# Input projection in 256-column units with seven half-size products for eight, and gates by exponential and logarithm

## The chip, the cores and the metric

One core of a Trainium2 chip runs the whole program. The metric is the device time of one execution in microseconds (us); three runs of the kernel before gave 1003.85, 1004.28 and 1004.38, median 1004.28.

Five engines run side by side, each in the order of its own queue: TensorE (PE, matmuls, with its weight loads shown as PEld), VectorE (DVE), ScalarE (ACT), GpSimd (POOL) and SyncE (SP), which issues most of the DMAs. Matmuls write to PSUM, eight banks of 128 x 512 float32 values; everything else lies in SBUF.

## The reference

One decoder layer on x of 512 tokens x 2048 columns, in float32. Sixteen heads of width 128 in three kinds: six forgetting (FoX), six stick-breaking, four differential ones with two maps each.

```
h = x @ w_in                      # 2048 x (16 heads x 4 x 128 + 6): q, k, v, gate of each head
FoX:            softmax(q k / sqrt(128) + c_t - c_s) v,  c = cumsum(log_sigmoid(ff + b_f))
stick-breaking: weights exp(log_beta + later sums of log(1 - beta)), strictly causal, times v
differential:   (softmax(q1 k1 - slope*dist) - lam * softmax(q2 k2 - slope*dist)) v, RMS norm
out = concat(heads * silu(gate)) @ w_out
x   = LayerNorm(2**0.25 * x + out) * ln_g + ln_b
```

## The kernel before, in words

Every product of two float32 matrices is made of three float32r passes (`mm3`, L104): each operand is split into a high and a low part (`split`, L113: ACT casts the high part, DVE subtracts it for the low part), and high x high, high x low, low x high are summed in PSUM.

The input projection runs over 16 column groups of 512 columns, for each quad of heads one with q and k of two heads, one with the values of four, one with the other q and k, one with four gates. A group runs over 8 weight chunks of two row tiles (256 x 512 values, `load_chunk`, L144), and a chunk over four accumulators (one PSUM bank each, tags `pj0` to `pj3`): this is a unit, 2 x 3 matmuls of 512 columns. For q, k and gates the weights are the stationary operand and x^T (`xh`, `xl`) is the moving one; for values it is the other way round, so that they come out by tokens.

The order of PE is the order of emission (`mm` pins it). Other work is put between units by a clock that counts them: `at_unit` (L175) files a step under a unit, `tick` (L178) runs what is due. `attend` (L595) files each head's steps: for the four blocks of 128 queries the scores (two PSUM tiles `psL`), eight to ten units later the transposes of the weights through the one PSUM tile `psT` (`transpose_w`, L536, evacuated by an ACT cast `pth` and a DVE subtraction `ptl`), then the weighted sum over values into the one tile `psO` (`weighted_v`, L548). Evacuations of a finished accumulator belong to `evac_qk`, `evac_diff`, `evac_v` and `evac_g`. The gate there is g / (1 + exp(-g)), with four reciprocals of 128 columns per head on DVE (L411). The engines other than PE get their order from a scheduler that lays the instructions out on an estimated timeline.

Weights are split two chunks ahead (`AHEAD`), through four raw tiles and three pairs of split tiles. Twelve of the sixteen gated heads go to DRAM and are read back during the last group (`load_mix`, L443). The output projection (four groups of 512 columns, the last one in another order so that the norms can start early) and the layer norm end the program.

Of the kernel before, what the change touches and what calls it, by code (L numbers as in the profile page):

```python
# [63 lines left out]
UNITS = NK // KC * 4        # matmul units (one accumulator, one weight chunk) in a column group  # L64
NRES = 3
AHEAD = 2                   # weight chunks split ahead of their products
# [3 lines left out]
def trunk(ctx, tc, x, w_in, b_f, lam_p, subln_g, w_out, ln_g, ln_b, out):  # L70
# [33 lines left out]
    def mm3(ps, ah, al, bh, bl, first, last, part=None):  # L104
        """ps += a^T b in three float32r passes, or one of them."""
# [6 lines left out]

    def split(hi, lo, src, scale=None):  # L113
        """hi + lo = src (* scale), each with at most 12 significant bits."""
        if scale is None:
            A.copy(hi, src)  # L116
            V.tensor_tensor(out=lo, in0=src, in1=hi.bitcast(F32), op=ALU.subtract)  # L117
# [8 lines left out]
    groups = []  # L126
    for quad in range(4):
        hq = ORDER[4 * quad:4 * quad + 4]
        for kind in ("qk", "v", "qk", "g"):
            if kind == "qk":  # L130
                hs = hq[:2] if len(groups) % 4 == 0 else hq[2:]
                cols = [head_cols(h)[0] for h in hs] + [head_cols(h)[1] for h in hs]
            else:
                hs = hq
                cols = [head_cols(h)[2 if kind == "v" else 3] for h in hs]
            groups.append((kind, hs, cols))
    NG = len(groups)
    NJ = NK // KC
    chunks = [(w1, g, j) for g in range(NG) for j in range(NJ)]
    chunks += [(w2, g, j) for g in range(NG, NG + 4) for j in range(NJ)]  # L140
    ready = {}
    RES = (NG + 3) * NJ + NRES       # from here on the parts stay resident

    def load_chunk(n):  # L144
        """Load and split rows of KC k-tiles of a column group's weights."""
        w, g, j = chunks[n]
        raw = wpool.tile([P, KC, 512], F32, tag="raw", bufs=4, name=f"raw{n}")
        if w is w1:
            for dst, src, wd in runs(groups[g][2]):
                nc.sync.dma_start(raw[:, :, dst:dst + wd], w[:, j * KC:(j + 1) * KC, src:src + wd])  # L150
        else:
            k0, c0 = ORDER[j * KC], (g - NG) * 512
            nc.sync.dma_start(raw, w[:, k0:k0 + KC, c0:c0 + 512])
        if n < RES:
            hi = wpool.tile([P, KC, 512], F32R, tag="whi", bufs=3, name=f"whi{n}")
            lo = wpool.tile([P, KC, 512], F32R, tag="wlo", bufs=3, name=f"wlo{n}")
        else:
            hi = fin.tile([P, KC, 512], F32R, name=f"whi{n}")
            lo = fin.tile([P, KC, 512], F32R, name=f"wlo{n}")
        if n < RES and not (j == AHEAD and g < NG):  # L160
            split(hi, lo, raw)
        else:
            pin(A.copy(hi, raw))
            pin(V.tensor_tensor(out=lo, in0=raw, in1=hi.bitcast(F32), op=ALU.subtract))
        ready[n] = (hi, lo)
# [17 lines left out]
    def run_group(g, acc, product, evac, after_chunk=None):  # L183
        """All units of a column group: product(n, kt, accumulator), then evac of each accumulator."""
        for j in range(NJ):
            n = g * NJ + j
            if n == 0:
                load_chunk(AHEAD)
                for k in range(KC):
                    for part in range(3):  # L190
                        for c in range(4):
                            if k == KC - 1 and part == 2:
                                tick()
                            product(ready[n], k, k, c, part)
                        if k == 0 and part == 0:
                            transpose_x(1)
                        if k == 1 and part < 2:
                            transpose_x(2 + part)
            for c in range(4) if n > 0 else ():
                if c == 0 and n + AHEAD < len(chunks) and n + AHEAD not in ready:  # L200
                    load_chunk(n + AHEAD)
                tick()
                for k in range(KC):
                    product(ready[n], k, j * KC + k, c)
                if j == NJ - 1:
                    evac(c, acc[c])
            del ready[n]
            if after_chunk is not None:
                after_chunk(j)

# [5 lines left out]
    # products of ones, read by nobody: they open TensorE's clock gate while the first loads run  # L216
# [10 lines left out]
    xh = [kx.tile([P, S], F32R, tag=f"h{kt}", name=f"xh{kt}") for kt in range(NK)]  # L227
    xl = [kx.tile([P, S], F32R, tag=f"l{kt}", name=f"xl{kt}") for kt in range(NK)]
# [4 lines left out]
    with ExitStack() as actx:  # L233
        at = actx.enter_context(tc.tile_pool(name="at", bufs=1))

        def wk(name):
            return at.tile([P, S], F32, tag="wk", bufs=8, name=name)
# [5 lines left out]
        xv = xf.rearrange("(tb p) c -> p tb c", p=P)  # L243
        xraw = []

        def load_x(c):
            xr = at.tile([P, NT, 512], F32, tag=("pth", "ptl")[c % 2], name=f"xr{c}")
            xraw.append(xr)
            if c > 0:
                x_part(c, 0, 256)  # L250
                x_part(c, 256, 512)

        def x_part(c, c0, c1):
            nc.sync.dma_start(xraw[c][:, :, c0:c1], xv[:, :, c * 512 + c0:c * 512 + c1])

        def transpose_x(kt):
            c, s = divmod(kt, 4)
            pt = (psL, psL, psT, psO)[s](f"xt{kt}")
            for tb in range(NT):
                transpose(pt[:, tb * P:(tb + 1) * P], xraw[c][:, tb, s * P:(s + 1) * P], ident)  # L260
            split(xh[kt], xl[kt], pt)

# [1 line left out]
        rel = const.tile([P, S], F32, name="rel")  # L264
        cmask = const.tile([P, S], F32, name="cmask")
# [3 lines left out]
        def constants():  # L269
            # distance rel[p, j] = p - j + 384, and the causal mask on the last 128 columns  # L270
            G.iota(rel, pattern=[[-1, S]], base=S - P, channel_multiplier=1,
                   allow_small_or_imprecise_dtypes=True)
            V.memset(cmask, 0.0)
            G.affine_select(out=cmask[:, S - P:], in_=cmask[:, S - P:], pattern=[[-1, P]], base=0,
                            channel_multiplier=1, compare_op=ALU.is_ge, fill=BIG)
            # lambda, on every partition
# [17 lines left out]
        def ff_start():  # L294
# [4 lines left out]
            # columns 0-5 the hi parts, 32-37 the lo parts: one pass over xh takes both  # L299
# [8 lines left out]
        def ff_products(k0):  # L308
# [4 lines left out]
            for kt in range(k0, k0 + 4):  # L313
                if kt == 0:
                    mm(ps[:32 + NF], wfs[:, kt, :], xh[kt], True, False)
                mm(ps[:NF], wfs[:, kt, :NF], xl[kt], False, False)
                if kt > 0:
                    mm(ps[:32 + NF], wfs[:, kt, :], xh[kt], False, kt == NK - 1)
# [10 lines left out]
            c = at.tile([P, S], F32, tag="mx", bufs=4, name="ffc")[:NF]  # L329
            V.tensor_tensor_scan(out=c, data0=e, data1=e, initial=0.0, op0=ALU.add, op1=ALU.min)  # L330
            nc.sync.dma_start(cd, c)
            ff["c"] = c

# [8 lines left out]
        qs, ks, vt, mixed = {}, {}, {}, {}  # L342

        def evac_qk(hs):
            h0 = hs[0]
            fox, sb = h0 < NF, NF <= h0 < NF + NS
            scale = HD ** -0.5 if sb else (-(HD ** -0.5) if fox else -((HD // 2) ** -0.5))

            def evac(c, ps):
                h = hs[c % 2]  # L350
                if not (fox or sb):
                    evac_diff(c, h, ps, scale)
                    return
# [441 lines left out]
```

## Time and profile before

| | |
|---|---|
| median of three runs | 1004.28 us (1003.85 to 1004.38) |
| the profiled execution, first to last instruction (span) | 1002.8 us |
| what lies around the span, against the median | 1.5 us |
| instructions | 12020 |
| granted TensorE clock, mean over the span | 0.995 |
| HBM read, written | 99.27 MB, 7.35 MB |

The profile is of one execution. Its own time is the span; the rest of the median is start and end outside the recorded instructions. A busy time is the union of an engine's instructions. PE's matmuls overlap each other in the record, so the distance between the starts of two of them says more than the length of one. An idle time stands in brackets or behind a bar, with the instruction that ended it.

### The profile page before, as it was taken

What the parts mean: (1) busy time and instruction counts of PE and PEld (TensorE: products, weight loads), DVE (VectorE), ACT (ScalarE), POOL (GpSimd) and SP (SyncE); (2) the same over time, 40 slices, a digit from 0 to 9 for tenths busy, and PEclk for the clock granted to TensorE, in tenths of its full rate; (3) what the DMA queues carried; (4) which work ended last, traced back from release to release, by engine and by line L of the source; (5) the groups of instructions that cost most, each with busy time, mean ns of one, the idle gap of its engine ahead of it and who ended that gap; (6) DMA issues with size and microseconds to landing.
All of it is one profiled execution on the core that took longest, in us unless ns stands there. A gap on an engine that the chain in (4) does not pass through costs nothing.

```text
span 1002.8 us, 12020 instructions
## 1 busy us (share of the span) xinstructions
PE 985.7 (98%) x4572; PEld 810.2 (81%) x4572; DVE 529.6 (53%) x869; ACT 377.6 (38%) x631; POOL 100.4 (10%) x130
## 2 busy tenths in 40 slices
PE   9999999999999999999999999999999999999994
PEld 7877888888888877877887888888888888888884
DVE  5433544459435465596466355833435675432548
ACT  3323543444335443444344333433435642121212
POOL 0000000013100000120000001401000001000026
PEclk9999999999999999999999999999999999999998
DMA  9432232224332222233333233333233424733203
GB/s 291 131 89 85 84 84 84 84 85 136 95 105 85 81 76 79 87 99 95 96 85 92 86 95 95 115 96 113 87 95 117 146 85 158 284 103 101 100 32 147
DMA packets 84818, 107.41 MB, mean 107 GB/s; under 512 B 7442, under 2 KB 61842, under 8 KB 84504
## 3 DMA queue, kind: packets, MB, share of 16 engines
q1 hardware_dynamic: 81112, 95.63, 31.4%
q10 hardware_dynamic: 3168, 9.44, 2.6%
q0 software_dynamic: 480, 1.57, 0.5%
q8 instruction: 36, 0.59, 0.2%
q14 instruction: 22, 0.18, 0.1%
HBM read 99.27 MB, written 7.35 MB: 106 GB/s over the span
## 4 chain that ended last, share of the span: by engine, by line
PE 94%; DVE 4%; DMA 1%; issue 0%; SPq 0%; ACT 0%
PE p L99 84%; PE l L99 3%; PE o L99 3%; PE pt L102 2%; DMA raw<-in_w_in_dram 1%; DVE y L730 1%; PE ffps L99 1%; PE xt L102 1%; DVE kl L380 0%; DVE wlo L117 0%; DVE y L712 0%; DVE lt L719 0%; DVE stt L696 0%; PE p_end L99 0%; ACT whi L116 0%
## 5 line engine op out<-in xcount | busy, mean ns | idle before, releaser
L117 DVE TENSOR_TENSOR wlo<-raw,whi 128x1024 fp32r<-128x1024 f32 x138 | 171.9, 1245 | 266.4 <-ACT whi L116 266.3
L99 PE MATMUL p<-xh,whi 128*128 128x512 f32 x768 | 307.2, 401 | 0.3 <-DVE kl L380 0.3
L99 PE MATMUL p<-xh,wlo 128*128 128x512 f32 x768 | 299.8, 392 | 0.0
L99 PE MATMUL p<-xl,whi 128*128 128x512 f32 x768 | 298.8, 390 | 0.8 <-DVE xl L117 0.8
L116 ACT CAST whi<-raw 128x1024 fp32r<-128x1024 f32 x138 | 145.2, 1052 | 268.9 <-PE p L99 189.5
L99 PEld LDWEIGHTS p<-xh,wlo 128*128 128x128 f32 x768 | 144.1, 188 | 31.5
L99 PEld LDWEIGHTS p<-xh,whi 128*128 128x128 f32 x768 | 144.5, 188 | 30.7 <-issue 2.6
L99 PEld LDWEIGHTS p<-xl,whi 128*128 128x128 f32 x768 | 144.4, 188 | 28.3 <-DVE xl L117 1.4
L99 PE MATMUL p<-whi,xh 128*128 128x512 f32 x256 | 101.7, 397 | 1.0 <-DVE kl L380 0.9
L99 PE MATMUL p<-whi,xl 128*128 128x512 f32 x256 | 100.1, 391 | 0.0
L99 PE MATMUL p<-wlo,xh 128*128 128x512 f32 x256 | 99.8, 390 | 0.0
L99 PE MATMUL p<-wlo,mh 128*128 128x512 f32 (+1 forms) x256 | 98.1, 383 | 0.0
L99 PE MATMUL p<-whi,mh 128*128 128x512 f32 (+1 forms) x256 | 98.0, 383 | 0.0
L99 PE MATMUL p<-whi,ml 128*128 128x512 f32 (+1 forms) x256 | 98.0, 383 | 0.0
L411 DVE RECIPROCAL ge<-ge 128x128 f32<-128x128 f32 x64 | 58.0, 931 | 0.4
L475 ACT ACTIVATE u<-u,m 128x128 f32<-128x128 f32 (+3 forms) x56 | 31.5, 562 | 70.8 <-DVE m L472 70.8
L99 PEld LDWEIGHTS p<-whi,xh 128*128 128x128 f32 x256 | 48.1, 188 | 12.4 <-issue 2.2
L99 PEld LDWEIGHTS p<-whi,xl 128*128 128x128 f32 x256 | 48.0, 188 | 10.5
L99 PEld LDWEIGHTS p<-whi,mh 128*128 128x128 f32 x256 | 48.1, 188 | 9.7
L99 PEld LDWEIGHTS p<-whi,ml 128*128 128x128 f32 x256 | 48.1, 188 | 9.6
L99 PEld LDWEIGHTS p<-wlo,mh 128*128 128x128 f32 x256 | 48.1, 188 | 9.5
L99 PEld LDWEIGHTS p<-wlo,xh 128*128 128x128 f32 x256 | 48.1, 188 | 9.3
(159 smaller groups left out, 973.8 us busy)
## 6 DMA issues: line engine op xcount, KB each, us to landing
raw<-in_w_in_dram SPq DMA_DIRECT2D x190, 256.0 KB, 3.0
raw<-in_w_in_dram SPq DMA_DIRECT2D x32, 512.0 KB, 3.7
raw<-in_w_out_dram SPq DMA_DIRECT2D x32, 512.0 KB, 3.7
xr<-in_x_dram SPq DMA_DIRECT2D x7, 512.0 KB, 6.2
out_dram<-y SPq DMA_DIRECT2D x14, 256.0 KB, 2.1
mixd<-mx SPq DMA_DIRECT2D x12, 256.0 KB, 2.3
mr<-mixd ACTq DMA_DIRECT2D x12, 256.0 KB, 3.6
y<-in_x_dram ACTq DMA_DIRECT2D x4, 768.0 KB, 8.4
```

The source lines that it names most:

```text
L99: pin(T.matmul(ps, lhs, rhs, start=start, stop=stop))
L102: pin(T.transpose(dst, src, idt))
L116: A.copy(hi, src)
L117: V.tensor_tensor(out=lo, in0=src, in1=hi.bitcast(F32), op=ALU.subtract)
L411: pin(V.reciprocal(ei, ei))
L475: A.activation(u[:, :n], u[:, :n], AF.Exp, bias=m, scale=-1.0, accum_out=sm)
L730: V.scalar_tensor_tensor(out=y[:, cs], in0=y[:, cs], scalar=r, in1=bb[:, cs], op0=ALU.mult, op1=ALU.add)
```

## The change

The projection keeps the weights as the stationary operand throughout and runs in 32 units of 256 columns: q, k, v and gate of each pair of heads. A unit has four weight chunks of four row tiles (512 x 256 values). The first pair's q and k are done together as before (`"f"` chunks, 8 of them); 30 units follow. In two of the four chunks (`SJ`, rows 0 to 1023) the product of a 2 x 2 block of weight halves with a 2 x 2 block of halves of x^T (rows by tokens) is formed from seven products of half size, in place of eight: `seven` makes the sums of weight blocks (one subtraction on POOL, two on DVE) and their splits, `x_sums` makes the sums of blocks of x^T once. Each half-size product is 2 row tiles x 3 passes of 256 columns; they go into halves of four banks (`BANK`) in the order `SEVEN`. Behind the second such chunk, `e` collects the sums that are shared, and at the unit's end each of the two heads' results is one more sum, `cc`. The other two chunks (`CJ`) are multiplied as before, 512 columns at a time.

Values now come out transposed, so `evac_v` turns them by four transposes per head through `psT`. The gate is g * exp(min(g, 0) - log(1 + exp(-|g|))): four ACT functions, one DVE and one POOL operation. The scaling of softmax weights moves from DVE to ACT, the ALiBi bias from DVE to POOL and ACT. The weighted sum goes by two halves of the queries. The raw tiles are three, shared with x (eight tiles of 256 columns); split tiles are six of 512 columns. Fourteen heads go through DRAM, and are read back within the last unit. The last pair's steps reach into the first group of the output projection.

```diff
+SJ = (0, 1)
+CJ = tuple(j for j in range(NK // 4) if j not in SJ)
+SEVEN = (1, 5, 7, 6, 2, 4, 3)
+BANK = {1: ("a", 0), 6: ("a", 1), 5: ("b", 0), 7: ("b", 1), 2: ("c", 0), 4: ("c", 1), 3: ("d", 0)}
+H2 = S // 2
...
+    def seven(n, raw):
+        b21, b22 = raw[:, 2:4, :P], raw[:, 2:4, P:]
+        t = wpool.tile([P, 4, 2, P], F32, tag="t", bufs=1, name=f"t{n}")
+        G.tensor_tensor(out=t[:, 0:2], in0=raw[:, :, P:].rearrange("p (b k) c -> p b k c", b=2),
+                        in1=raw[:, 0:2].rearrange("p k (b c) -> p b k c", b=2), op=ALU.subtract)
+        V.tensor_tensor(out=t[:, 2], in0=b22, in1=t[:, 0], op=ALU.subtract)
+        V.tensor_tensor(out=t[:, 3], in0=b21, in1=t[:, 2], op=ALU.subtract)
+        fa = part_tiles(f"a{n}", [P, 4, P])
+        split(*fa, raw[:, :, :P])
+        fb = part_tiles(f"b{n}", [P, 2, 2, P])
+        split(*fb, t[:, 0:2])
+        fc = part_tiles(f"c{n}", [P, 2, 2, P])
+        split(*fc, t[:, 2:4])
+        fd = [wpool.tile([P, 2, P], F32R, tag=f"wd{i}", bufs=2, name=f"wd{i}_{n}") for i in range(2)]
+        split(*fd, b22)
...
+        def evac_v(h, s, c):
+            pt = psT(f"vp{h}")
+            for kb in range(NT):
+                transpose(pt[:, kb * P:(kb + 1) * P], c[:, kb * P:(kb + 1) * P], ident)
+            hi = at.tile([P, NT, HD], F32R, tag=f"vh{s}", name=f"vh{h}")
+            lo = at.tile([P, NT, HD], F32R, tag=f"vl{s}", name=f"vl{h}")
+            split(hi, lo, pt.rearrange("p (kb d) -> p kb d", d=HD))
...
+        def silu(h, c):
+            e = wk(f"ge{h}")
+            A.activation(e, c, AF.Abs)
+            A.activation(e, e, AF.Exp, scale=-1.0)
+            A.activation(e, e, AF.Ln, bias=1.0)
+            V.scalar_tensor_tensor(out=e, in0=c, scalar=0.0, in1=e, op0=ALU.min, op1=ALU.subtract)
+            A.activation(e, e, AF.Exp)
+            G.tensor_tensor(out=c, in0=c, in1=e, op=ALU.mult)
...
+        for p, (ha, hb) in enumerate(PAIRS):
+            if p < len(PAIRS) - 1:
+                attend(ha, 64 * p + 34, 6, 8, 5)
+                attend(hb, 64 * p + 60, 6, 8, 5)
+            else:
+                attend(ha, 64 * p + 34, 5, 8, 5)
+                attend(hb, 64 * p + 52, 5, 8, 5)
...
+        for u in range(2, NU):
+            for pos, j in enumerate(SJ + CJ):
+                load_ahead(n)
+                if j in SJ:
+                    for m, pr in enumerate(SEVEN):
+                        if m % 2 == 0:
+                            tick()
...
+                        for i in range(2):
...
+                            mm3(dst, wp[pr][0][:, i], wp[pr][1][:, i], bh, bl,
+                                pos == 0 and i == 0 and half == 0,
+                                j == SJ[-1] and i == 1 and b in "ab" and half == 1)
+                    if j == SJ[-1]:
+                        e = at.tile([P, 6, H2], F32, tag="e", name=f"e{u}")
+                        A.copy(e[:, 0:2], pb["a"].rearrange("p (b t) -> p b t", b=2))
+                        V.tensor_tensor(out=e[:, 2], in0=e[:, 0], in1=e[:, 1], op=ALU.add)
...
+                else:
+                    for c in range(2):
+                        for k in range(4):
+                            if k % 2 == 0:
+                                tick()
...
+                            elif kind == 2:
+                                at_unit(clock[0] + 2 + c, lambda h=h, c=c, cc=cc: evac_v(h, c, cc))
+                            else:
+                                at_unit(clock[0] + 2 + 3 * c, lambda h=h, cc=cc: silu(h, cc))
```

The clock still ticks every six full-size matmuls; in a sevenfold chunk it ticks with every second product. The steps of the order at three places follow. The first is PE before, in the second q and k group of the first quad of heads, where the second block of head 10's weights is transposed into `pt10_1` (`rs` are the weights, `whi`, `wlo` the split weights of the projection, `p5` and so on its accumulators by group).

```order
L99 MATMUL p5_2_2127<-whi46_2290,xh13_101 128x512
L99 MATMUL p5_2_2127<-wlo46_2291,xh13_101 128x512
L99 MATMUL p5_2_2127<-whi46_2290,xl13_117 128x512
L102 MATMUL pt10_1_2414<-ident_73,rs10_1_2322 128x128 x2
L99 MATMUL p5_3_2128<-whi46_2290,xh12_100 128x512
L99 MATMUL p5_3_2128<-wlo46_2291,xh12_100 128x512
L99 MATMUL p5_3_2128<-whi46_2290,xl12_116 128x512
```

Between the transposes into `psT` and the next use of `psT` lie, there and everywhere before, the products of at least one unit. The second is PE in the change, at the same two transposes, which now stand at the start of unit 11, the gates of heads 10 and 11 (`vp10` is the `psT` tile for the values of head 10, `c10_0` those values transposed, `xa0`, `xs0_0` the blocks and sums of x^T, `wha`, `whb` the parts of the weight blocks).

```order
L106 MATMUL p10d_3137<-x15l_131,wh43_1_3148 128x512
L106 MATMUL p10d_3137<-x15h_130,wl43_1_3149 128x512
L109 MATMUL pt10_1_3348<-ident_73,rs10_1_3233 128x128 x2
L109 MATMUL vp10_3353<-ident_73,c10_0_3305 128x128 x4
L106 MATMUL p11a_3362<-xa0h_88,wha44_3207 128x256
L106 MATMUL p11a_3362<-xa0l_89,wha44_3207 128x256
L106 MATMUL p11a_3362<-xa0h_88,wla44_3208 128x256
```

The value transposes stand directly behind the transposes of the weights, in the same PSUM tile; it is so for heads 6, 8, 10, 12, 14, 0 and 2, the first heads of the first seven pairs. The third is DVE in the change around its last read of `pt10_1` (`wlb45`, `wlc45` splits of the next sevenfold chunk, `e10_2`, `rs10_2` the third block of head 10, `c10_0`, `c10_1` the sums that end unit 10).

```order
L201 TENSOR_TENSOR t45_3273<-raw45_3271,t45_3273 128x256
L202 TENSOR_TENSOR t45_3273<-raw45_3271,t45_3273 128x256
L798 TENSOR_TENSOR c10_0_3305<-e10_3196,p10c_3124 128x512
L121 TENSOR_TENSOR wlb45_3282<-t45_3273,whb45_3281 128x512
L550 SCALAR_TENSOR_TENSOR e10_2_3311<-l10_2_3307,e10_2_3311 128x384
L121 TENSOR_TENSOR wlc45_3286<-t45_3273,whc45_3285 128x512
L121 TENSOR_TENSOR ptl10_0_3253<-pt10_1_3348,pth10_0_3252 128x2x128
L554 SCALAR_TENSOR_TENSOR rs10_2_3317<-e10_2_3311 128x384
```

The last read of `pt10_1` stands behind a block of the next scores and a split of the next chunk; before, one `wlo` split of a whole chunk stood for the six operations of a sevenfold one.

## Rows read from the trace of the kernel before

**Rows 1.** The page, part 1: busy time (share of span) and instructions by engine.
```profile
PE 985.7 (98%) x4572; PEld 810.2 (81%) x4572; DVE 529.6 (53%) x869; ACT 377.6 (38%) x631; POOL 100.4 (10%) x130
```

**Rows 2.** The page, part 4: shares of the chain that ended last, by engine.
```profile
PE 94%; DVE 4%; DMA 1%; issue 0%; SPq 0%; ACT 0%
```

**Rows 3.** Timeline of PE (start us, us, line, operation): projection, first and last.
```profile
265.78 0.44 PE L99 MATMUL p<-whi,xh 128*128 128x512 f32 x1
...
279.26 0.40 PE L99 MATMUL p<-whi,xl 128*128 128x512 f32 x1
```

**Rows 4.** Timeline of PE and of its weight loads (PEld), last column group.
```profile
954.70 0.28 PE L99 MATMUL p_end<-whi,mh 128*128 128x256 f32 x1
954.70 0.19 PEld L99 LDWEIGHTS p_end<-wlo,mh 128*128 128x128 f32 x1
...
955.42 0.40 PE L99 MATMUL p<-whi,mh 128*128 128x512 f32 x1
```

**Rows 5.** Timeline of PE around four transposes in the projection.
```profile
122.98 0.60 PE L102 MATMUL pt<-ident,rs 128*128 128x128 f32 x4
123.33 0.47 PE L99 MATMUL p<-xh,whi 128*128 128x512 f32 x1
123.64 0.39 PE L99 MATMUL p<-xl,whi 128*128 128x512 f32 x1
```

**Rows 6.** Timeline of PE: one head's weighted sum, from its first matmul.
```profile
263.92 0.39 PE L99 MATMUL o<-pth,vh 128*128 128x512 f32 x1
...
265.14 0.28 PE L99 MATMUL o<-pth,vh 128*128 128x256 f32 x1
```

**Rows 7.** Timeline at three places: the matmul behind two transposes, DVE's last read.
```profile
188.84 0.38 PE L102 MATMUL pt<-ident,rs 128*128 128x128 f32 x2
188.97 0.48 PE L99 MATMUL p<-xh,whi 128*128 128x512 f32 x1
...
190.12 0.41 DVE L117 TENSOR_TENSOR ptl<-pt,pth 128x256 fp32r<-128x256 f32 x1
...
640.74 0.48 PE L99 MATMUL p<-xh,whi 128*128 128x512 f32 x1
...
641.43 0.42 DVE L117 TENSOR_TENSOR ptl<-pt,pth 128x256 fp32r<-128x256 f32 x1
...
777.56 0.48 PE L99 MATMUL l<-kh,qh 128*128 128x512 f32 x1
...
781.09 0.41 DVE L117 TENSOR_TENSOR ptl<-pt,pth 128x256 fp32r<-128x256 f32 x1
```

**Rows 8.** Groups (xcount | busy us, mean ns | idle before); last, one tile's.
```profile
L117 DVE TENSOR_TENSOR wlo<-raw,whi 128x1024 fp32r<-128x1024 f32 x138 | 171.9, 1245 | 266.4 <-ACT whi L116 266.3
L411 DVE RECIPROCAL ge<-ge 128x128 f32<-128x128 f32 x64 | 58.0, 931 | 0.4
L117 DVE TENSOR_TENSOR vl<-p,vh 128x512 fp32r<-128x512 f32 x16 | 11.0, 689 | 8.0 <-ACT vh L116 8.0
L117 DVE TENSOR_TENSOR ptl<-pt,pth 128x256 fp32r<-128x256 f32 x16 | 6.6, 411 | 3.0 <-ACT pth L116 2.8
L414 POOL TENSOR_TENSOR g<-g,ge x16: 1288/1299/2144, 223.1 to 839.7; 128x512 f32<-128x512 f32 x16
```

**Rows 9.** Timeline of PE: the longest wait in the steady stream.
```profile
463.27 0.47 PE L99 MATMUL p<-whi,xh 128*128 128x512 f32 x1 [0.87 <-DVE kl L380]
```

**Rows 10.** Timeline of POOL and DVE: a multiplication and a split that overlap.
```profile
244.35 1.35 POOL L432 TENSOR_TENSOR mx<-mx,g 128x512 f32<-128x512 f32 x1
244.48 2.31 DVE L117 TENSOR_TENSOR wlo<-raw,whi 128x1024 fp32r<-128x1024 f32 x1
```

**Rows 11.** Stretch 400:560: busy PE, PEld, DVE, ACT, POOL; then of `wlo` alone.
```profile
400.00:560.00 160.00, 158.99 (x727) 128.22 (x726) 103.22 (x207) 67.20 (x123) 13.56 (x9) 1.00 0.31 91
400.00:560.00 160.00, 78.36 (x201) 37.76 (x201) 31.69 (x25) 1.00 0.31 91
```

More of the change, by code (lines that the diff above doesn't have):

```diff
@@ L61, in runs @@
     return out
-UNITS = NK // KC * 4
+SJ = (0, 1)
+CJ = tuple(j for j in range(NK // 4) if j not in SJ)
 NRES = 3
 AHEAD = 2
+T0 = 32
+TU = 16
+PAIRS = [(ORDER[2 * p], ORDER[2 * p + 1]) for p in range(NK // 2)]
+SEVEN = (1, 5, 7, 6, 2, 4, 3)
+BANK = {1: ("a", 0), 6: ("a", 1), 5: ("b", 0), 7: ("b", 1), 2: ("c", 0), 4: ("c", 1), 3: ("d", 0)}
+H2 = S // 2
 @with_exitstack
@@ L137, in trunk @@
[L137 to L150, printed above, removed]
-        else:
[L152 to L165, printed above, removed]
@@ new lines, in trunk, with raw_tile, part_tiles @@
+    NJ = NK // KC
+    NU = 4 * len(PAIRS)
+    chunks = [("f", 0, j) for j in range(NJ)]
+    chunks += [("u", u, j) for u in range(2, NU) for j in SJ + CJ]
+    N_OUT = len(chunks)
+    chunks += [("o", g, j) for g in range(4) for j in range(NJ)]
+    ready = {}
+    RES = N_OUT + 3 * NJ + NRES
+    def raw_tile(name, shape):
+        return wpool.tile(shape, F32, tag="raw", bufs=3, name=name)
+    def part_tiles(name, shape, pool=None):
+        if pool is not None:
+            return (pool.tile(shape, F32R, name=f"wh{name}"), pool.tile(shape, F32R, name=f"wl{name}"))
+        return (wpool.tile(shape, F32R, tag="wh", bufs=6, name=f"wh{name}"),
+                wpool.tile(shape, F32R, tag="wl", bufs=6, name=f"wl{name}"))
@@ new lines, in first_cols, with load_chunk @@
+    def first_cols(k0, k1):
+        return [(i * 256, w1[:, k0:k1, c:c + 256]) for i, c in enumerate(head_cols(PAIRS[0][0])[:2])]
+    def load_chunk(n):
+        kind, g, j = chunks[n]
+        if kind == "u":
+            raw = raw_tile(f"raw{n}", [P, 4, 256])
+            c0 = head_cols(PAIRS[g // 4][0])[g % 4]
+            nc.sync.dma_start(raw, w1[:, 4 * j:4 * j + 4, c0:c0 + 256])
+            if j in SJ:
+                ready[n] = seven(n, raw)
+            else:
+                halves = [part_tiles(f"{n}_{i}", [P, 2, 256]) for i in range(2)]
+                for i in range(2):
+                    split(*halves[i], raw[:, 2 * i:2 * i + 2])
+                ready[n] = [(halves[k // 2][0][:, k % 2], halves[k // 2][1][:, k % 2]) for k in range(4)]
+            return
+        raw = raw_tile(f"raw{n}", [P, KC, 512])
+        if kind == "f":
+            for dst, src in first_cols(j * KC, (j + 1) * KC):
+                nc.sync.dma_start(raw[:, :, dst:dst + 256], src)
+        else:
+            k0, c0 = ORDER[j * KC], g * 512
+            nc.sync.dma_start(raw, w2[:, k0:k0 + KC, c0:c0 + 512])
+        ready[n] = []
+        for k in range(KC):
+            if n >= RES and slots_left:
+                hi, lo = kx_pair(slots_left.pop(0), [P, 512], f"w{n}_{k}")
+            else:
+                hi, lo = part_tiles(f"{n}_{k}", [P, 512], fin if n >= RES else None)
+            if n < RES and not (n == AHEAD):
+                split(hi, lo, raw[:, k])
+            else:
+                pin(A.copy(hi, raw[:, k]))
+                pin(V.tensor_tensor(out=lo, in0=raw[:, k], in1=hi.bitcast(F32), op=ALU.subtract))
+            ready[n].append((hi, lo))
@@ L181, in tick, with load_ahead @@
         clock[0] += 1
[L183 to L209, printed above, removed]
+    def load_ahead(n):
+        if n + AHEAD < len(chunks) and n + AHEAD not in ready:
+            load_chunk(n + AHEAD)
     ident = const.tile([P, P], F32, name="ident")
@@ L312, in ff_products @@
             ps = ff["ps"]
[L313 to L318, printed above, removed]
+            for kt in ff["order"][k0:k0 + 4]:
+                for cs, hi, lo in x_parts(kt):
+                    first = kt == ff["order"][0]
+                    if first:
+                        mm(ps[:32 + NF, cs], wfs[:, kt, :], hi, True, False)
+                    mm(ps[:NF, cs], wfs[:, kt, :NF], lo, False, False)
+                    if not first:
+                        mm(ps[:32 + NF, cs], wfs[:, kt, :], hi, False,
+                           kt == ff["order"][-1] and cs.stop == S)
             if k0 + 4 < NK:
@@ L332, in ff_products @@
             ff["c"] = c
+        ff["order"] = [kt for kt in range(NK) if kt in xh] + [kt for kt in range(NK) if kt not in xh]
         def ff_end():
@@ new lines, in trunk, with bank, product @@
+        at_unit(T0 + 20, ff_end)
+        def bank(u, b):
+            return ps_p.tile([P, 512], F32, tag=f"pj{b}", name=f"p{u}{b}")
+        acc = [bank(0, b) for b in "abcd"]
+        def product(n, k, c, part=None):
+            kt = chunks[n][2] * KC + k
+            hi, lo = ready[n][k]
+            ps = slice(c * P, (c + 1) * P)
+            for cs, bh, bl in x_parts(kt):
+                mm3(acc[c][:, cs], hi[:, ps], lo[:, ps], bh, bl, kt == 0 and cs.start == 0,
+                    kt == NK - 1 and cs.stop == S, part)
@@ new lines, in out_product, with out_chunk @@
+        def out_product(n, k, kt, t, c0, ps):
+            ts = slice(t * P, (t + 1) * P)
+            cs = slice(c0, c0 + ps.shape[-1])
+            hi, lo = ready[n][k]
+            mm3(ps, mh[kt][:, ts], ml[kt][:, ts], hi[:, cs], lo[:, cs], kt == 0, kt == NK - 1)
+        def out_chunk(g, j, acc, last):
+            n = N_OUT + g * NJ + j
+            load_ahead(n)
+            for t in range(NT):
+                tick()
+                for k in range(KC):
+                    out_product(n, k, j * KC + k, t, 0, acc[t])
+                if last is not None and j == NJ - 1:
+                    last(t)
+            del ready[n]
@@ L669, in trunk @@
+        acc0 = [bank("o0", b) for b in "abcd"]
+        for j in range(NJ):
+            out_chunk(0, j, acc0, None)
         for u in sorted(events):
```

365 lines of the change are left out of this document (205 added, 160 removed).

## The prediction, made before the change was timed

> **What bounds the kernel now.** I read the page's first part, then the chain, then stretches of the timeline. TensorE (PE) is busy for 985.7 of 1002.8 us, VectorE (DVE) for 529.6, ScalarE (ACT) for 377.6, GpSimd (POOL) for 100.4 [rows 1]; 94% of the chain that ended last lies on PE [rows 2]. The reader is to see that nothing but PE's own stream sets the time, so that every term below is either matmuls taken out of that stream or put into it, or a place where the stream has to wait. A recorded matmul is longer than its turn, because matmuls overlap; what counts is the distance from start to start. Sixty 512-column matmuls of the projection start at 265.78 to 279.26 [rows 3]: 13.48 us for 59 turns, 0.2285 us each. Six 256-column matmuls of the last column group, each with a weight load of its own, take 954.70 to 955.42 [rows 4]: 0.120 us each. So a half-size product costs 0.120/0.2285 = 0.525 of a full one, not 0.5.
>
> **The sum.** All of it is against the profiled execution, span 1002.8 us; the median of the runs is 1004.28, so 1.5 us lie around the span and stay.
>
> 1. Seven products. A unit of 256 columns had 96 matmuls of 512. Now two of its four weight chunks take 7 x 2 x 3 = 42 matmuls of 256 columns in place of 24 of 512: 42 x 0.120 = 5.04 us against 24 x 0.2285 = 5.48, a gain of 0.44. Thirty units have two such chunks: -26.6 us. Counting columns alone (7/8 of 60 x 5.48) one would expect -41; the fixed part of each turn eats the rest.
> 2. Halves where there were wholes. In the first eight chunks the products over four of the sixteen row tiles go in two halves, 48 products of 512, and so does one matmul in each of the 30 units and eight of the forget gate's: 86 times 2 x 0.120 - 0.2285, +1.0 us.
> 3. The value heads come out transposed and are turned back: 16 groups of four 128x128 transposes. Such a group holds the stream from 122.98 to 123.33, and the next matmul takes 0.31 in place of 0.23 [rows 5]: 0.43 us each, +7.0 us.
> 4. The weighted sum over values goes by halves of the queries. Today a head's twelve matmuls run 263.92 to 265.78, 1.86 us, of which 265.14 to 265.78 is three of 256 and three of 128 columns, so 0.093 for one of 128 [rows 3, 6]. Now twelve of 256 and six of 128: 1.44 + 0.56 = 2.00. Sixteen heads: +2.2 us.
>
> The stream shrinks by 26.6 - 10.2 = 16.4 us. Now the waits.
>
> 5. A collision. Pairs of heads have one PSUM tile, `psT`, for transposes. In seven of the eight pairs the order puts the four transposes of the pair's first value head directly behind the two of the weights' second block; both write `psT`. PE, which runs in order, must stand until ACT and DVE have copied the first result out. Nothing covers it: the whole product stream is queued behind. The trace of before has the same step without a waiter. At 188.84 two transposes start, the next matmul at 188.97, and DVE is through with the tile at 190.12 + 0.41 = 190.53: PE would have stood 1.56 us. The best of these stretches gives 641.43 + 0.42 - 640.74 = 1.1 and the worst, with other work ahead on ACT and DVE, 781.09 + 0.41 - 777.56 = 3.9 [rows 7]. I take 1.5, since in the new order ACT's and DVE's copy stands behind the next scores' work as it does in the first example: 7 x 1.5 = +10.5 us, bounds 7.7 and 27. In the eighth pair the two places lie one unit (about 1.4 us) apart: +0.5.
> 6. DVE's and ACT's new work, on the side. In every unit DVE splits three 512-column tiles and three 256-column ones per sevenfold chunk, four 512s in the plain ones, and joins the products with three operations and two sums. By the rows of such shapes, 0.689 and 0.411 us [rows 8], that is 2 x 3.30 + 2.76 + 1.51 + 1.38 = 12.25 us for a unit, where it was four splits of 1.245, 5 us. Against that the 64 reciprocals of the gates go, 58 us. ACT gets some 400 instructions more (the small casts, the gates' functions, the scaling of the softmax); at its present mean, 377.6 us for 631 [rows 1], that is under 240 us, and 620 of 1000 is no bound. I cost it and the gates at nothing; the cover is the two chunks, some 10 us, that the weights are split ahead, and without it the late one is the next weight cast, 0.6 us each time.
>  The heavy place is the differential heads. In 400 to 560 DVE is busy for 103.2 of 160 us, 31.7 of it weight splits [rows 11] and 16 x 0.93 = 14.9 reciprocals [rows 8], so 56.6 remain, 35 per 100 us. The 25 splits stand for 25 x 24 x 0.2285 = 137 us of products, so attention takes 14% of PE's time there and a unit lasts some 21.05/0.86 = 24.5 us. DVE's 12.25 of that is 50 per 100: together 85. That is under 100, but near the stretch around 460 where DVE was full and PE stood 0.87 us for a key split [rows 9]. I add one more such wait: +1.0 us; between nothing and what the first rival says.
> 7. At nothing: the ring of raw weight tiles is three deep for four and x now shares it. SP issues fewer, larger loads (120 of 512 KB for 222 entries), each two chunks before its use; cover gone, a load of some 4 us would show once. Fourteen of the mixed heads are read back in the last unit in place of twelve over a whole group, on ACT's queue, behind which the last casts wait: up to 2 us, kept for the range. The end after the last matmul is untouched.
>
> Sum: -26.6 + 1.0 + 7.0 + 2.2 + 10.5 + 0.5 + 1.0 = -4.4. Span 998.4, median **999.9 us**.
>
> **Rivals.**
>
> *DVE becomes the bound (slower).* The sevenfold chunks give POOL 60 subtractions of 512 columns, 1.3 us at their shortest [rows 8], on data in SBUF. What they do to DVE can be seen once before: POOL's multiplication starts at 244.35 for 1.35 us, DVE's split at 244.48, and the split, 1.245 us on the mean [rows 8], takes 2.31 [rows 10]: it stood for nearly all of POOL's instruction. If each of the 60 costs DVE its whole length, the 8 in 100 us add 10.6 to the 85: 96. In-order queues at that load do not keep pace; at one wait of 0.9 us per 25 us over the 200 us of differential heads and half as many over 300 us of the stick-breaking ones, 7 + 5 us come on top, less the 1.0 that I have: 1011 us. It decides from the point where DVE's work for a unit, waits included, passes the unit's 24.5 us. Against it: POOL can as well be the one that waits, and each collision of step 5 gives DVE 1.5 us to catch up. 20%.
>  The Trainium skill, "SBUF — State Buffer", section "SBUF: two separate sides", says that the pair of ports which VectorE and GpSimd share is an exclusive lock held for the full instruction, taken by a DVE operation with two SBUF inputs and by GpSimd; the trace agrees in the 2.31 us above.
>
> *The collision is cheap.* If ACT and DVE are idle when the transposes end, each wait is the 1.1 of the best stretch, and the extra DVE wait does not come: 999.9 - 2.8 - 1.5 = 995.6 us. For it: the stall itself frees these two engines. 25%.
>
> *Half-size products pay a full weight load.* Each load is recorded with 0.19 us [rows 4]. Were it not overlapped, a sevenfold chunk would take 42 x 0.19 = 8.0 us for 5.48, 60 times +2.5: 1150 us. Against it: in the six of [rows 4] the loads stand 0.12 apart, each beginning while the one before is still shown. 2%.
>  The Trainium skill, "Perfetto Trace Analysis", section "Identifying the Most-Contended Engine", takes the busy share of LDWEIGHTS as the sign of how full TensorE is; by that the 81% of now leaves no room for 1,300 more loads, and the trace's 0.12 us speaks against it.
>
> **How the numbers follow.** My forecast (waits of step 5 near 1.5) has 45%, the cheap collision 25%, DVE as the bound 20%, the weight loads 2%; the remaining 8% are waits near 2.7 at the collisions, +8 us, 1008. What a measurement can tell from no change is 0.2%, 2 us. Under 1002.3 lie the cheap collision and three quarters of the forecast, which is uncertain by some 4 us: 0.59. Within 2 us of 1004.3 are the rest of the forecast and a part of the dearer waits: 0.17. Above: 0.24, most of it DVE. The range must take in the cheap collision with 256-column turns of 0.118 (5 us less, 990) and reach DVE as the bound: 990 to 1011.
>
> **What would show it.** In the new profile: 256-column products at 0.120 us from start to start (0.19 would confirm the third rival); PE idle for 1 to 3 us in front of `vp` transposes, seven times, released by DVE's `ptl` copy; DVE busy for 650 to 750 us with its fullest slices between 400 and 600 us, and PE's other idle time there under 3 us in sum. PE busy near 970. If idle time of PE is spread over many rows that wait for DVE's `wl` splits, DVE is the bound and I am wrong. If PE's busy time falls by less than 10 us, the price of a half-size product is wrong.

## The result, and the profile after

The changed kernel takes 1013.94 us (1013.44 to 1014.15), the kernel before beside it 1004.32; the ratio is 1.0097, 95% interval 1.0083 to 1.0111. It is 9.6 us slower where 4.4 less was forecast, and 2.9 us above the range. The profiled execution has a span of 1011.7 us against the forecast's 998.4: 13.3 us to explain.

The page of the kernel after, parts 1 and 4, answering to [rows 1, 2]:

```profile
PE 975.5 (96%) x5898; PEld 864.6 (85%) x5898; DVE 697.0 (69%) x1311; ACT 517.7 (51%) x1044; POOL 201.8 (20%) x214
...
PE 92%; DVE 4%; ACT 1%; DMA 1%; issue 1%; SPq 0%; POOL 0%; ACTq 0%; DVEq 0%; POOLq 0%
```

PE is busy 10.2 us less and yet the span is 8.9 us longer: idle time has come in. Which, the waits of PE in the kernel after tell (engine, output and line, released by; us in total, times, longest):

```profile
PE vp L109 <- DVE ptl L121: 11.7, 7, 2.1
PE pt L109 <- DVE u L579: 2.7, 1, 2.7
PE pt L109 <- DVE ptl L121: 2.3, 1, 2.3
PE p0a L106 <- ACT xb0h L126: 2.2, 1, 2.2
PE pt L109 <- DVE vl L121: 1.7, 1, 1.7
```

The first row is the collision of step 5, seven times. The others are a differential head's first block at 480.1 us, two places in the last unit (811.5 and 795.5 us) and the start. The seventh collision, on the timeline of the kernel after (PE, then ACT, then DVE):

```profile
686.90 0.38 PE L109 MATMUL pt<-ident,u 128*128 128x128 f32 x2
689.39 0.66 PE L109 MATMUL vp<-ident,c 128*128 128x128 f32 x4 [2.11 <-DVE ptl L121]
...
690.68 0.41 PE L106 MATMUL p27b<-xs_0h,whb 128*128 128x256 f32 x1
690.89 0.41 PE L106 MATMUL p27b<-xs_0l,whb 128*128 128x256 f32 x1
...
687.40 0.72 ACT L530 ACTIVATE d<-cb,ncq 128x512 f32<-128x512 f32 x1
688.02 0.60 ACT L536 ACTIVATE u<-u,r 128x384 f32<-128x384 f32 x1
688.53 0.35 ACT L126 CAST pth<-pt 128x256 fp32r<-128x256 f32 x1
...
688.91 0.43 DVE L121 TENSOR_TENSOR ptl<-pt,pth 128x256 fp32r<-128x256 f32 x1 [0.52 <-ACT pth L126]
```

PE stands behind the two transposes until ACT, which first makes the next block's bias and scales another, casts the tile, and DVE subtracts. Then something shows that no term had: from 690.68 on the products start 0.213 us apart, not 0.120 (a turn is the distance from start to start; these are the slow turns below). The stretches of PE there (length, busy and count, granted clock, DMA share, GB/s):

```profile
688.00:690.00 2.00, 0.61 (x5) 1.00 0.06 20
690.00:691.00 1.00, 1.00 (x9) 0.74 0.63 160
691.00:692.00 1.00, 1.00 (x7) 0.50 0.16 61
692.00:693.00 1.00, 1.00 (x6) 0.50 0.08 16
693.00:694.00 1.00, 1.00 (x7) 0.56 0.00 0
694.00:696.00 2.00, 2.00 (x19) 1.00 0.00 0
```

The granted clock fell to half (2.4 to 1.2 GHz) about 1 us after PE went on, and came back while PE worked: 15 turns, each 0.093 us longer, 1.4 us. It happened three times: here, behind the 1.7 us wait at 795.5 (15 turns), and at the start, there within the wait itself (22 turns, 2.1 us). Behind the 2.1 us stall at 591.8, the 2.3 us one at 811.5 and the 2.7 us one at 480.1 it did not. The Trainium skill, "TensorE: Matmul & The Clock Gate", Part 1, says that idleness closes the gate to half rate; here single stalls of about 2 us, with PE 96% busy over the span, were followed by it in some places and not in others.

The start, on the timeline of the kernel after (PE, ACT, DVE), with two stretches of PE:

```profile
6.01 0.35 PE L106 MATMUL p0a<-xa0h,wh 128*128 128x256 f32 x1 [0.62 <-DVE wh L686]
8.52 0.58 PE L106 MATMUL p0a<-xb0h,wh 128*128 128x256 f32 x1 [2.15 <-ACT xb0h L126]
...
4.76 0.37 ACT L126 CAST xa0h<-xt 128x256 fp32r<-128x256 f32 x1 [2.03 <-PE xt L109]
8.10 0.37 ACT L126 CAST xb0h<-xt 128x256 fp32r<-128x256 f32 x1 [2.96 <-DVE xa0l L121]
...
7.30 0.43 DVE L686 CAST wh<-raw 128x512 fp32r<-128x512 f32 x1 [0.71 <-DMA raw<-in_w_in_dram]
7.64 0.42 DVE L121 TENSOR_TENSOR xa0l<-xt,xa0h 128x256 fp32r<-128x256 f32 x1
...
7.00:8.00 1.00, 0.00 (x0) 0.90 0.83 291
8.00:9.00 1.00, 0.48 (x2) 0.50 0.19 66
```

The first tile of x goes in halves. ACT's cast of the second half waited for DVE's subtraction of the first, and that stood in DVE's queue behind a weight tile still on its way.

**The ledger, against the forecast's span** (waits, plus slow turns at 0.093): collisions 11.7 + 1.4, forecast 10.5: +2.6. Last unit 1.7 + 2.3 + 1.4, forecast 0.5: +4.9. Differential head 2.7, forecast 1.0: +1.7. Start 2.2 + 0.6 + 2.1, less the 0.8 that the kernel before waits there: +4.1. Together 13.3, the whole miss; so the product stream came out as forecast, to within about 1 us (the ledger leaves out 1.1 us of waits for `kl` that only the kernel before has).

### The profile page after: what moved, and what is told of

The parts are those of the page before. It is cut to its first block, busy times and chain, and to the rows that moved or that the text cites. A ratio compares the mean times of both kernels' runs of the same rounds, so it can differ in the third digit from the quotient of the medians.

```text
span 1011.7 us, 15878 instructions
## 1 busy us (share of the span) xinstructions
PE 975.5 (96%) x5898; PEld 864.6 (85%) x5898; DVE 697.0 (69%) x1311; ACT 517.7 (51%) x1044; POOL 201.8 (20%) x214
## 4 chain that ended last, share of the span: by engine, by line
PE 92%; DVE 4%; ACT 1%; DMA 1%; issue 1%; SPq 0%; POOL 0%; ACTq 0%; DVEq 0%; POOLq 0%
PE o L106 10%; PE l L106 3%; PE pt L109 2%; PE p0a L106 1%; PE p0c L106 1%; PE p0b L106 1%; PE p0d L106 1%; PE po0a L106 1%; PE po0d L106 1%; PE po0c L106 1%; PE po0b L106 1%; PE po2d L106 1%; PE po2c L106 1%; PE po2b L106 1%; PE po2a L106 1%; DMA mr<-mixd 1%
## 5 line engine op out<-in xcount | busy, mean ns | idle before, releaser
L121 DVE TENSOR_TENSOR wl<-raw,wh 128x512 fp32r<-128x512 f32 x186 | 128.4, 703 | 111.3 <-ACT wh L126 110.6
L126 ACT CAST wh<-raw 128x512 fp32r<-128x512 f32 x186 | 113.6, 618 | 159.7 <-PE po2d L106 33.1
L199 POOL TENSOR_TENSOR t<-raw 128x512 f32<-128x512 f32 x60 | 86.6, 1443 | 331.1 <-DVE wlc L121 244.6
L121 DVE TENSOR_TENSOR wlc<-t,whc 128x512 fp32r<-128x512 f32 x60 | 41.5, 692 | 44.4 <-ACT whc L126 44.2
L126 ACT CAST whc<-t 128x512 fp32r<-128x512 f32 x60 | 37.0, 617 | 57.3 <-PE p5d L106 4.4
L121 DVE TENSOR_TENSOR wla<-raw,wha 128x512 fp32r<-128x512 f32 x60 | 54.8, 913 | 12.5 <-ACT wha L126 7.6
L121 DVE TENSOR_TENSOR wlb<-t,whb 128x512 fp32r<-128x512 f32 x60 | 46.7, 779 | 19.3 <-ACT whb L126 19.2
L201 DVE TENSOR_TENSOR t<-raw,t 128x256 f32<-128x256 f32 x60 | 40.6, 677 | 25.2 <-POOL t L199 25.1
L126 ACT CAST wha<-raw 128x512 fp32r<-128x512 f32 x60 | 37.3, 621 | 21.6 <-DMA raw<-in_w_in_dram 2.6
L126 ACT CAST whb<-t 128x512 fp32r<-128x512 f32 x60 | 37.0, 616 | 12.7 <-PE p22d L106 3.6
L121 DVE TENSOR_TENSOR ptl<-pt,pth 128x128 fp32r<-128x128 f32 (+1 forms) x64 | 31.0, 485 | 11.6 <-ACT pth L126 11.2
L126 ACT CAST pth<-pt 128x128 fp32r<-128x128 f32 (+1 forms) x64 | 27.0, 422 | 18.1 <-PE pt L109 14.4
L202 DVE TENSOR_TENSOR t<-raw,t 128x256 f32<-128x256 f32 x60 | 30.0, 501 | 1.0
```

What stands on the lines that cost most here:

```text
L199: G.tensor_tensor(out=t[:, 0:2], in0=raw[:, :, P:].rearrange("p (b k) c -> p b k c", b=2), in1=raw[:, 0:2].rearrange("p k (b c) -> p b k c ...
L201: V.tensor_tensor(out=t[:, 2], in0=b22, in1=t[:, 0], op=ALU.subtract)
L202: V.tensor_tensor(out=t[:, 3], in0=b21, in1=t[:, 2], op=ALU.subtract)
```

## The experiments

Times are medians; the kernel before gave 1003.9 to 1004.3 beside them.

**The collisions taken away.**

```
- at_unit(clock[0] + 2 + c, lambda ...: evac_v(h, c, cc))
+ at_unit(clock[0] + 4, lambda ...: evac_v(h, c, cc))
```

> The value transposes of both heads of a pair are filed two units later for the first head (one for the second), so that they stand two units behind the second weight block's transposes and two ahead of the third's. Theory A (the stalls are the price of one PSUM tile and nothing else): the seven waits in front of vp, 12.8 us in sum in the changed kernel's trace, go, and with them the 16 slow turns behind the one at 689 us (16 x 0.093 = 1.5 us): 12.8 to 14.3 us less, about 1000 us. Theory B (DVE is too full, and the stalls are where it catches up): the waits come back in front of other transposes or of products that wait for weight splits; less than 6 us are gained, above 1008 us.

999.53 us (997.75 to 1000.4), 14.4 less than the changed kernel; ratio to before 0.9953 (0.9938 to 0.9968). The sequence alone decides between slower and faster. Waits of PE in this run:

```profile
PE pt L109 <- DVE u L579: 2.7, 1, 2.7
PE vp L109 <- DVE ptl L121: 2.6, 1, 2.6
PE p0a L106 <- ACT xb0h L126: 1.6, 1, 1.6
```

The seven are gone; the 2.6 us are in the last pair, whose steps stand closer, so that the edit makes a new collision there. The last unit stays at 31.6 us for 32.3, so the gain is not made there: 11.9 of the 13.8 us by which the profile is shorter lie in the seven pairs of units with a collision, though slow turns now follow the 2.7 us wait. Theory B falls. (The 12.8 us of the expectation, and the 1.84 and 2.50 of one further below, count from start to start, less a turn; the 11.7, 1.7 and 2.3 above count idle time alone.)

**The start, by other quarters of the contraction.**

```
- SJ = (0, 1)
+ SJ = (2, 3)
- at_unit(11 + 8 * n + 3 * i, lambda j=j, i=i: x_sums(j, i))
+ at_unit(20 + 8 * n + 3 * i, lambda j=j, i=i: x_sums(j, i))
```

> The sevenfold chunks are the third and fourth quarter of the contraction in place of the first two, so that the first row tiles of x are whole tiles and the first chunk's products are full-size. Theory A (the start lost time to the second half-tile's cast, which ACT makes only when DVE is through with the first half): the 2.15 us wait at 8.5 us and the 28 products behind it that ran at half the granted clock (28 x 0.093 = 2.6 us) go; 4 to 5 us less, about 1009.5 us. Theory B (the start waits for loads whatever the tiles): the wait moves to the next weight tile and under 1.5 us are gained, about 1013.

1021.16 us (1016.53 to 1025.18): 7 us worse, against both theories. The 2.15 us wait is gone, as in theory A, but in the profile the sums of x come late instead: PE waits 1.5 us for one in the first unit behind the `"f"` chunks, 0.6 and 0.7 for halves at 49 to 51 us, with slow turns behind, and 3.5 in the last unit for 2.3. The profile is of the shortest execution (1016.53); the executions spread over 9 us, and why so wide stays open.

**The heads read back one by one.**

```
- load_mix(kt)
+ at_unit(clock[0] + 2 * (kt - 2 * pos), lambda kt=kt: load_mix(kt))
```

> The fourteen mixed heads are read back one every two units, from the last unit into the first group of the output projection, in place of seven behind each sevenfold chunk of the last unit. Theory A (the casts and subtractions of the heads read back stand ahead of the attention's copies on ACT and DVE): the waits at 795 and 812 us (1.84 and 2.50 us) shrink to under 0.5 each, and the 16 slow turns behind the first (1.5 us) go; 4 to 6 us less, about 1009 us. Theory B (the last pair's steps are filed too close for the one PSUM tile, whatever else runs): both waits stay, under 1.5 us gained.

1008.46 us, 5.5 less. The wait at 812 is gone, the one at 795 is 0.7 us, and no slow turns follow; the last unit lasts 27.4 us for 32.3. These 4.9 us are the edit's; in this profile the start, which it does not touch, also ran without slow turns. Theory A. The wait that is left:

```profile
PE pt L109 <- DVE vl L121: 0.7, 1, 0.7
```

The timeline of the kernel after shows what stood in the way (ACT, then DVE: `m` are heads read back):

```profile
807.94 0.61 ACT L126 CAST m13h<-mr 128x512 fp32r<-128x512 f32 x1
808.46 0.50 ACT L530 ACTIVATE d<-cb,ncq 128x256 f32<-128x256 f32 x1
808.87 0.56 ACT L126 CAST pth<-pt 128x512 fp32r<-128x512 f32 x1
...
808.89 0.68 DVE L121 TENSOR_TENSOR m12l<-mr,m12h 128x512 fp32r<-128x512 f32 x1
809.49 0.68 DVE L121 TENSOR_TENSOR m13l<-mr,m13h 128x512 fp32r<-128x512 f32 x1
...
810.71 0.69 DVE L121 TENSOR_TENSOR ptl<-pt,pth 128x512 fp32r<-128x512 f32 x1
```

**One sevenfold chunk in place of two.**

```
- SJ = (0, 1)
+ SJ = (0,)
- if u == NU - 1 and j in SJ:
-     for kt in range(7 * pos, min(7 * pos + 7, NK - 2)):
+ if u == NU - 1 and pos < 3:
+     for kt in range(*((0, 7), (7, 11), (11, NK - 2))[pos]):
```

> Only the first quarter of the contraction is formed from seven products; the second is multiplied as before, 30 chunks with 24 full-size products in place of 42 half-size ones. Theory A (a half-size product costs 0.120 us, and DVE's work hides behind PE): 30 chunks dearer by 0.44 (at 0.2285 us a full-size product) to 0.52 us (at 0.2318, the mean without stalls), so 13 to 16 us more, about 1028 us. Theory B (DVE is the bound: with one sevenfold chunk per unit it has some 1.7 us less to do in each): the stalls shrink by as much as the products grow, between 1010 and 1018 us.

1025.17 us (1022.61 to 1027.69), 11.2 more; between the theories, since stalls changed too (the differential head's is 1.1 us for 2.7). Most units without a wait are 0.39 to 0.53 us longer.

**The start, by the order of the casts.**

```
  for cs, hi, lo in x_parts(kt):
-     split(hi, lo, pt[:, cs])
+     A.copy(hi, pt[:, cs])
+ for cs, hi, lo in x_parts(kt):
+     low(lo, pt[:, cs], hi)
```

> The changed kernel with one edit: for a tile of x that goes in halves, ACT's casts of both halves stand ahead of DVE's two subtractions. Theory A (the second half's cast waits for DVE's subtraction of the first, which stands in DVE's queue behind the first weights' casts): the second product no longer waits 2.15 us at 8.5 us, the products that follow do not fall to half the granted clock, and about 3 us (1 to 5) are gained: about 1011 us. Theory B (the halves themselves, or the clock's state at that moment whatever PE waits for, make the start slow): under 1 us.

1013.44 us (1011.76 to 1016.77): nothing in the median. The 2.15 us wait and the slow turns at the start are gone, but in this profile slow turns follow three other stalls (480, 593 and 692 us, about 1.5 us each), one of them the very 2.1 us stall that had none in the first profile; the last unit's longest wait is 3.3 us for 2.3, and the first chunks have new waits of 0.9 to 1.0 us. Not conclusive by itself; it is measured again below.

**All repairs together**: casts first, heads one by one, and

```
- at_unit(clock[0] + 2 + c, lambda ...: evac_v(h, c, cc))
+ at_unit(clock[0] + ((4, 4) if u < NU - 4 else (3, 6))[c], lambda ...: evac_v(h, c, cc))
- at_unit(u0 + i * every + lag, lambda i=i: transpose_w(h, i, ws.pop(i)))
+ at_unit(u0 + i * every + lag + (2 if i == 0 and h >= NF + NS else 0),
+         lambda i=i: transpose_w(h, i, ws.pop(i)))
```

> All repairs together: value transposes two units behind the second and two ahead of the third weight block's (in the last pair two behind the second block's and two behind the third's), casts of both halves first, mixed heads read back one every two units, and the first weight block's transposes of differential heads filed two units later. Theory A (the stalls were independent places on PE's path): from 1013.9 us the seven collisions and the slow turns behind them go (-14.4 as measured for that edit alone), the 2.6 us that this edit left in front of the last pair's transposes, the last unit's 4.9 us, the 2.7 us in front of the differential head's first block, and about 3 at the start: about 986 us (983 to 991), 1.8% faster than the kernel before. Theory B (with the gaps closed DVE no longer keeps pace): DVE's share rises above 71%, waits for splits or copies of 0.5 us and more spread over many places, and the time stays above 994.

990.11 us (989.85 to 990.22), ratio to before 0.9862 (0.9847 to 0.9877): 1.4% faster than the kernel before. The page, part 1:

```profile
PE 970.2 (98%) x5898; PEld 859.2 (87%) x5898; DVE 697.7 (71%) x1311; ACT 516.0 (52%) x1044; POOL 200.6 (20%) x214
```

No stretch of slow turns is left and no wait behind the first chunks is over 0.6 us; the longest:

```profile
PE vp L109 <- ACT ncq L409: 0.6, 1, 0.6
```

Theory A; it does not quite reach 986. Counted from the first product of a unit to that of the next, the whole difference of the two profiles, 23.3 us, lies where the edits are: 15.7 in the seven pairs of units with a collision (one of them holds the differential head's wait), 5.8 in the last two units, 1.8 before the first unit of seven products.

**POOL's subtraction on DVE**, all else as in the run before:

```
- G.tensor_tensor(out=t[:, 0:2], in0=raw...
+ V.tensor_tensor(out=t[:, 0:2], in0=raw...
```

> As the run with all repairs, but the sevenfold chunks' first subtraction of weight blocks runs on DVE in place of POOL: 60 x 0.69 = 41 us more work for DVE, less what POOL's instruction costs DVE's beside it (60 x (0.913 - 0.69) and 60 x (0.677 - 0.41), 29 us, by the means in the changed kernel's trace). Theory A (DVE hides behind PE, whichever of the two engines subtracts): within 3 us of the run with all repairs. Theory B (the two engines' overlap is what makes DVE late): faster by over 3 us. Theory C (DVE is near its bound): slower by over 5 us.

989.92 us, no difference. The groups after (first fence) and in this run (second):

```profile
L199 POOL TENSOR_TENSOR t<-raw 128x512 f32<-128x512 f32 x60 | 86.6, 1443 | 331.1 <-DVE wlc L121 244.6
L121 DVE TENSOR_TENSOR wla<-raw,wha 128x512 fp32r<-128x512 f32 x60 | 54.8, 913 | 12.5 <-ACT wha L126 7.6
L201 DVE TENSOR_TENSOR t<-raw,t 128x256 f32<-128x256 f32 x60 | 40.6, 677 | 25.2 <-POOL t L199 25.1
```

```profile
L199 DVE TENSOR_TENSOR t<-raw 128x512 f32<-128x512 f32 x60 | 41.2, 687 | 2.9 <-DMA raw<-in_w_in_dram 1.8
L121 DVE TENSOR_TENSOR wla<-raw,wha 128x512 fp32r<-128x512 f32 x60 | 42.5, 708 | 1.0 <-ACT wha L126 1.0
L201 DVE TENSOR_TENSOR t<-raw,t 128x256 f32<-128x256 f32 x60 | 25.8, 431 | 0.6
```

DVE does 41 us more and is busy only 11 us more (708.8): much of the rest had been its own operations held up beside POOL's, as the lengths of the last two groups show. The Trainium skill, "SBUF — State Buffer", section "SBUF: two separate sides", says that a GpSimd operation that reads SBUF and a DVE operation with two SBUF inputs exclude each other from the ports that they share, for a whole instruction; the trace agrees in these lengths. In this kernel it costs no time, because DVE hides behind PE. Theory A.

**The gates alone, in the kernel before** (lines shortened; filed at one unit in place of five).

```
- pin(V.tensor_scalar_max(e, s, -87.0)); A.activation(e, e, AF.Exp, scale=-1.0)
- pin(V.tensor_scalar_add(e, e, 1.0)); pin(V.reciprocal(ei, ei))   # four times 128 columns
+ A.activation(e, s, AF.Abs); A.activation(e, e, AF.Exp, scale=-1.0)
+ A.activation(e, e, AF.Ln, bias=1.0)
+ V.scalar_tensor_tensor(out=e, in0=s, scalar=0.0, in1=e, op0=ALU.min, op1=ALU.subtract)
+ A.activation(e, e, AF.Exp)
```

> The kernel before with one part of the change alone: the gates through absolute value, exponential, logarithm and exponential on ACT and one DVE operation, filed at one unit, in place of the four reciprocals of 128 columns on DVE. Theory A (off the path): DVE's busy time falls by some 60 us, ACT's rises by some 30, the time stays within 1 us of 1004.1. Theory B (the reciprocals were part of what held up the differential heads at 460 us): 1 to 2 us faster.

1002.59 us for 1003.92, ratio 0.9987 (0.9977 to 0.9996): 1.3 us faster, DVE at 472.3 us. The wait of [rows 9] shrinks to 0.3. Theory B, narrowly.

**One collision put back into the repaired kernel.**

```
- ((4, 4) if u < NU - 4 else (3, 6))[c]
+ ((2, 4) if u == 26 else (4, 4) if u < NU - 4 else (3, 6))[c]
```

> The kernel with all repairs, and one collision put back: in the seventh pair alone the first value head's transposes stand directly behind the second weight block's, as in the changed kernel, where PE stood 2.11 us there and the 16 turns behind it ran at half the granted clock. Theory A (a stall costs its own length and, in some executions, slow turns behind it): 990.1 + 2.1 = 992.2 us in the executions without slow turns, 993.7 in those with them; a median of 992 to 994. Theory B (the stall is given back, because DVE and ACT catch up in it): within 0.7 us of 990.1.

994.09 us (992.36 to 995.03), 4.0 more, just above the range of theory A; theory B falls. In the profile PE waits 2.1 us and 13 slow turns follow:

```profile
675.93 0.96 PE L109 MATMUL vp<-ident,c 128*128 128x128 f32 x4 [2.10 <-DVE ptl L121]
...
676.00:678.00 2.00, 2.00 (x11) 0.54 0.38 131
678.00:680.00 2.00, 2.00 (x13) 0.61 0.02 4
```

The two units that it lies between last 50.8 us for 47.0. A collision costs about twice its wait when the clock falls. That it falls in some executions only would fit the spread of 2.7 us (the two longer executions have a mean granted clock of 0.994, the two shorter 0.995 and 0.996), but only one was profiled, so this is not shown.

**One sevenfold chunk, without the stalls**, in the repaired kernel:

```
- SJ = (0, 1)
+ SJ = (0,)
```

The fourteen heads are filed from the first chunk on, still one every two units.

> The kernel with all repairs, but with one sevenfold chunk per unit in place of two: 30 chunks with 24 full-size products for 42 half-size ones, without the stalls that blur the same comparison in the changed kernel. Theory A (the saving is what the turns give: 24 x 0.2285 - 42 x 0.120 = 0.44, or with 0.2318 for a full-size turn 0.52): 13 to 16 us more than the run with all repairs, 1003 to 1006 us. Theory B (columns alone count, 12 of 96 full-size products per chunk pair): 30 x 0.68 = 20 us more, 1010. Theory C (the longer work of DVE in sevenfold chunks eats part of the saving even here): under 11 us more.

1005.92 us, 15.8 more. The projection behind the first chunks grows by 17.0 us in the profiles (751.9 for 734.9), of which some 3 are waits that the other order brings (1.3 us once in front of `pt`, 1.5 more in front of `vp`): 14 for 30 chunks, 0.47 each. Most units without a wait are 0.39 to 0.52 us longer. Theory A, near the forecast's 0.44; counted columns (3 x 0.2285 = 0.69) are refuted, and so is DVE's share.

**The start repair alone taken back, in the repaired kernel.**

```
+ split(hi, lo, pt[:, cs])
- A.copy(hi, pt[:, cs])
- low(lo, pt[:, cs], hi)
```

> The kernel with all repairs but the one at the start: the second half-tile's cast on ACT waits again for DVE's subtraction of the first. It measures that repair where nothing else stalls, since the run with that repair alone was blurred by slow turns elsewhere. Theory A (a wait of about 2 us before the second product, and some 20 to 28 products of 256 columns behind it at half the granted clock): 990.1 + 2 to 4.5, 992 to 994.6 us. Theory B (the start is bound by the first loads, and the wait only moves): within 1 us of 990.1.

991.87 us, 1.8 more, between the theories: the wait is 2.1 us and 11 slow turns follow, but the repaired start has waits of its own (0.4 to 0.5 us each for `xa0l`, `x3l`, `x8l`).

## Why the prediction was wrong, by its steps

1. **Seven products: right.** 256-column turns are 0.120 us, and a sevenfold chunk saves 0.47 us, for 0.44. (The third rival's 1150 us is a slip: 60 x (8.0 - 5.04) on top of 999.9 is 1176. Nothing else rests on it.)
2. **Halves, value transposes, weighted sum (steps 2 to 4): right together.** The repaired kernel, nearly without waits, has a span of 988.4 us; the forecast's stream alone gives 1002.8 - 16.4 = 986.4. No run separates the three.
3. **Step 5, the collision: the mechanism right, the size too small.** Place, number, releaser are as said; 11.7 us of waits for 10.5. I took 1.5 us each from a place of the stick-breaking heads (they gave 1.3 to 1.4); differential heads gave 1.6, the FoX heads 2.1, where ACT makes the bias of the next block ahead of the cast (at 687.40 above). For the eighth pair I had 0.5; it gave 1.7, but 0.7 with the heads read back one by one, so most of that belongs to step 7.
4. **Step 6: DVE's extra wait was 2.7, not 1.0**; and the gates, at nothing, gain 1.3 us by themselves. DVE was not the bound: the first rival is refuted by the run with all repairs, where DVE is 71% busy and PE hardly waits, and by the run without POOL's subtraction, which is no faster.
5. **Step 7, "At nothing": this is the step that failed.** It held the last unit at nothing in the sum and at "up to 2 us" in the range; it cost 5.4 us of waits and slow turns, and the experiment took 4.9 off it. It left out the start (4.9 us of waits and slow turns; the repair, which leaves smaller waits there, is worth 1.8). I named the queue of the heads read back, ACT's, and "the last casts" behind it, but not who stands behind their casts and subtractions: the copies of the last pair's attention on ACT and DVE, for which PE waits.
6. **No step had the clock.** 4.9 us of slow turns follow from stalls, in three places.

Steps 5 to 7 miss 2.6, 1.7 and 9.0 of 13.3 us; the slow turns are within these. The signs named beforehand mostly came true (seven waits in front of `vp`, 0.120 us, DVE at 697 us), since none of them looked at the start or the last unit.

## What to carry to other kernels

On an engine that is 98% busy, price a reordering by who now stands directly behind whom on a shared buffer, at the start and the end as well as in the steady part. Count a stall of TensorE of about 2 us as up to twice its length (4.0 us for 2.1 here). When a change is slower, look for its few long waits before giving up the arithmetic: here two numbers in a filing call were worth 14 us and turned 1% slower into 0.5% faster.

## What was not expected of the hardware

The granted clock fell to half behind stalls of 1.7 to 2.7 us in a stream otherwise full, and once behind two of 0.6 and 0.7 us (the run with other quarters), for 8 to 16 turns in the steady part (1.2 to 1.6 us), and not each time: the 2.1 us stall at 592 us was followed by slow turns in one profile and by none in another, and the longest of all, 3.5 us in the last unit of the run with other quarters, by none. Runs with long stalls often spread more (2.7 us with one put back) than the repaired kernel (0.4 us), but not always: the changed kernel itself spread 0.7 us. What decides is not settled here.
